# Some subtractions moved from VectorE to GpSimd, half loads paired in one buffer, and four copies issued later, in a one-core encoder layer on Trainium2

## The chip, the cores and the metric

The kernel runs on one core of one Trainium2 chip. The metric is the device time of one execution in microseconds (us). Three runs of the kernel before took 1076.27, 1076.62 and 1076.83; the median is 1076.62. Engine names are those of the profile: PE is TensorE's matmul, PEld its weight load, DVE is VectorE, ACT is ScalarE, POOL is GpSimd, SP is SyncE, which here only issues DMAs. PSUM is the memory that PE accumulates into, in banks of 128 x 512 floats; SBUF is the memory of the other tiles.

## The reference

One encoder layer over 1024 tokens with 1024 features, in float32. The input is normed and projected; the columns feed two token mixers side by side (group A: windowed grouped-query attention with a sink; group B: neighbourhood attention on a 16 x 64 grid). Each mixer's output is normed and both go through one output projection, with a residual. Then comes a gated MLP with 2816 hidden features, and a final norm. What the change touches is mostly the MLP's first half:

```python
def conv_gated_mlp(h, w_gate, w_up, conv_w, conv_b, w_down):
    g = jnp.einsum('bsd,df->bsf', h, w_gate)
    u = jnp.einsum('bsd,df->bsf', h, w_up)
    g = lax.conv_general_dilated(g, conv_w[:, None, :], ..., feature_group_count=D_FF) + conv_b
    return jnp.einsum('bsf,fd->bsd', jax.nn.silu(g) * u, w_down)
...
    h = h + jnp.einsum('bse,ed->bsd', mix, w_out[l])
    hn = rmsnorm(h, norm_ffn[l])
    h = h + conv_gated_mlp(hn, w_gate[l], w_up[l], conv_w[l], conv_b[l], w_down[l])
```

## The kernel before

**Precision by splitting.** Each float32 operand is split into a high part, rounded by ACT (`whi`, `hg`), and a low part, the rest, which VectorE subtracts (`wlo`, the second half of `hg`). A product of two operands is three matmuls: high x high, high x low and low x high (`group`, L957: L959, L960, L961; in the attention part `block`, L169). Weights come by a DMA on SP's queue into a tile `raw`; `split_w` (L943) makes the halves: L948 on ACT, L949 on VectorE. Inputs of the MLP are split by `operand` (L963: L966 on ACT, L967 on VectorE).

**Fewer products.** The MLP's products are blocked 2 x 2: tokens in two halves of 512, the 1024 features in two halves of four blocks of 128 (`K1` is blocks 0 to 3, `K2` blocks 4 to 7). Seven products of blocks replace eight, so sums and differences of the blocks are needed. `at(k, h)` is block k, half h, of the normed input. Of the first four blocks VectorE computes, in place, by `sub` (L998), the four sums that the names `t1` to `t4` stand for: t1 (L1181) and t2 (L1191) into `at(k, 1)`, then in one loop t3 (L1198) into `at(k, 0)` and t4 (L1199) into `at(k, 1)`. The last loop has eight subtractions of 128 x 512.

**Units.** A unit (class `Gated`, L1090) is one tile of 128 hidden features, gate and up together. It has seven products of 12 matmuls each: p1 and p2 into bank x, p5 and then p3 into bank y, p6, p7 and p4 into bank z. Where a second product goes into the same bank, it accumulates onto the first, so the instruction that reads the bank between them has to be done: L1100 and L1105 on ACT for x, L1110 and L1121 on VectorE for y, L1117, L1134 and L1139 on VectorE for z. The centred convolution is L1127 on ACT and L1128 and L1129 on VectorE, SiLU is L1130, the product of gate and up L1140.

**The head.** The first four units (`FO[:HEAD]`; here units 0 to 3) are run product by product: p1 and p2 of each, then p5 of all four (L1193), p6 of all four (L1200), p3, p7 and p4. Their weights come one product at a time (`head_weights`, L1002): a half of w_gate or of w_up, 256 KB, by `load_raw` (L952) into a tile `raw`, of which there are three of 512 KB size; a half load uses one whole tile. s1, s2, s4 and s3 are combinations of the halves and "22" is a half as it is. `sub` forms them in the tiles `ws`.

**The loop.** The other units (L1290; here unit 4, unit 5 and so on) go one after the other: p1, p5, p4 of the unit before, p6, p2, p3, convolution, p7. The steps of the next unit's weights (class `Weights`, L1045) stand between the products; its two loads are of 512 KB.

**Keeping.** When a unit's gate and up are multiplied, `keep` (L1153) stores the tile `c` of 512 KB to DRAM by a DMA on ACT's queue (L1155); `sums` (L1159) does the same for combinations of a pair of units. They are read back for the last part, the product with w_down.

**The output projection.** In the attention part the projections are jobs that fill PE between the attention's steps. A job's `load` is called one job ahead and `load_rest` at its twelfth step (`REST`, L757). `OutA` (L591) is the output projection of group A, eight jobs; its `load` fetches 256 KB and splits them at once (`load_w`, L166: L162 on ACT, L163 on VectorE), and its `load_rest` does nothing.

**What sets the order.** PE's instructions stand in the order of the program text (L128). Those of ACT, VectorE, GpSimd and SP are put in order by a scheduler when the program is built, by what it expects them to take; `behind` (L145) forbids it to put an instruction ahead of a named one, and `tc.high_priority` moves some forward. Each engine then works its list strictly in order, and a DMA is issued by the engine on whose queue it stands. A tile taken from a pool waits until the readers of its last user are done; `op` has 14 tiles (`c` and `cv` among them), `raw` three.

Of the kernel before, what the change touches and what calls it, by code (L numbers as in the profile page):

```python
# [13 lines left out]
F32 = mybir.dt.float32  # L14
F32R = mybir.dt.float32r
AF = mybir.ActivationFunctionType
ALU = mybir.AluOpType
# [3 lines left out]
KT = D // 128  # L21
NB = S // 128
HALF = 512
# [30 lines left out]
def hybrid_layer(tc, xT, w_first, w_in, w_out, w_gate, w_up, w_down, small, sink, rpb, consts, rope, out):  # L54
    nc = tc.nc
    with ExitStack() as ctx:
# [40 lines left out]
        for name, dst, n in (("h", his, 2), ("h", his, 2), ("l", los, 2), ("l", los, 2), ("w", None, 2)):  # L97
            t = flat(big(name, "mix", F32R)[:, :], n)
# [44 lines left out]
        mark = {}  # L143

        def behind(*names):  # L145

            stack = ExitStack()
            for n in names:
                stack.enter_context(tc.issue_after(mark[n].ins))
            return stack  # L150

        def fetch_w(src):

            raw = wpool.tile([128, 4, 128], F32, name="raw", tag="raw", bufs=2)
            nc.sync.dma_start(raw, src)
            return raw

        def halve_w(raw, held=False):

            hi, lo = (wpool.tile([128, 4, 128], F32R, name=n, tag=n) for n in ("whi", "wlo"))  # L160
            with behind(*["high", "rest"] * held):
                mark["weights"] = nc.scalar.activation(hi, raw, AF.Copy)  # L162
                mark["weights low"] = nc.vector.tensor_tensor(lo, raw, f32(hi[:, :, :]), op=ALU.subtract)  # L163
            return [(hi[:, j, :], lo[:, j, :]) for j in range(4)]

        def load_w(src):  # L166
            return halve_w(fetch_w(src), True)
# [422 lines left out]

        class OutA:  # L591
            def __init__(self, d):
                self.d = d

            def load(self):
                self.w = load_w(w_out[self.d, :, 0:4, :])

            def load_rest(self):
                pass

            def run(self):
                d = self.d
# [72 lines left out]
        t = quarters(big("f", "mix"))  # L675
# [5 lines left out]
        for part in range(3):  # L681
            for p, ps in zip(first, banks):
                w, x = p.w[0], xg[0]
# [129 lines left out]
        for g in range(2):  # L813
            for b in range(NB):
                q, t = unit_window(g, b)
# [53 lines left out]
        for u in range(len(flat)):  # L869
            q, t, need, kind = flat[u]  # L870
# [81 lines left out]
        def load_raw(src, n):  # L952
            raw = fpool.tile([128, n, 128], F32, name="raw", tag="raw", bufs=3, padded_shape=[128, KT, 128])
            nc.sync.dma_start(raw, src)
            return raw

        def group(ps, ws, xs, first, last):  # L957
            for i, (w, x) in enumerate(zip(ws, xs, strict=True)):
                nc.tensor.matmul(ps, w[0], x[0], start=first and i == 0, stop=False, skip_group_check=True)  # L959
                nc.tensor.matmul(ps, w[0], x[1], start=False, stop=False, skip_group_check=True)  # L960
                nc.tensor.matmul(ps, w[1], x[0], start=False, stop=last and i == len(ws) - 1, skip_group_check=True)  # L961
# [33 lines left out]
        HEAD = 4  # L995
        FH = FT // 2
        FO = [f for k in range(FH) for f in (k, k + FH)]
        sub = lambda o, x, y: nc.vector.tensor_tensor(o, x, y, op=ALU.subtract)  # L998

        wsum = [fpool.tile([128, 4, 128], F32, name="ws", tag="tt", bufs=6) for _ in range(HEAD)]  # L1000

        def head_weights(i, name):  # L1002
            f, t = FO[i], wsum[i]
            if name == "s1":
                u = load_raw(w_up[f], KT)
                nc.vector.tensor_tensor(t, u[:, 0:4], u[:, 4:8], op=ALU.add)
            elif name == "s2":
                g = load_raw(w_gate[f, :, 0:4], 4)
                sub(t, t, g)
            elif name == "s4":  # L1010
                g = load_raw(w_gate[f, :, 4:8], 4)
                sub(t, g, t)
            elif name == "s3":
                g, u = load_raw(w_gate[f, :, 0:4], 4), load_raw(w_up[f, :, 0:4], 4)
                sub(t, g, u)
            else:
                t = load_raw(w_up[f, :, 4:8], 4)
            W[f, name] = split_w(t, 4)

        for h in range(2):  # L1020
# [69 lines left out]
        class Gated:  # L1090
# [11 lines left out]
            def p2(self):  # L1102
                group(self.x, W[self.f, "12"], B[2, 1], False, True)
                self.gs = self.gs or big("gs", "mix")
                nc.scalar.activation(self.gs[:, 0:HALF], self.x, AF.Copy)  # L1105

            def p5(self):
                self.y = bank("y", self.tags[0])
# [27 lines left out]
            def p4(self):  # L1136
                group(self.z, W[self.f, "22"], B["t4"], False, True)
                u = self.c
                nc.vector.tensor_tensor(u[:, 0:HALF], self.z, u[:, 0:HALF], op=ALU.add)  # L1139
                nc.vector.tensor_tensor(u, u, self.cv, op=ALU.mult)  # L1140
                k = self.f % FH
                if self.f < FH:
                    first_of[k] = u
                    sub(u[:, HALF:S], u[:, HALF:S], u[:, 0:HALF])
                    keep(u, ("11", k), ("t1", k))
                else:
                    keep(u, ("21", k), ("22", k))


        FH = FT // 2  # L1150
        X, first_of = {}, {}

        def keep(t, *names):  # L1153
            d = dram.tile([128, HALF * len(names)], F32, name="x", tag="x" + "_".join(f"{n}{k}" for n, k in names))
            nc.scalar.dma_start(d, t)  # L1155
            for i, name in enumerate(names):
                X[name] = d[:, i * HALF:(i + 1) * HALF]
# [37 lines left out]
            head_weights(i, "s2")  # L1195
        B[2, 2] = [operand(at(k, 1), "op") for k in K2]
        for k in K1:
            sub(at(k, 0), at(k, 1), at(k, 0))  # L1198
            sub(at(k, 1), at(k + 4, 0), at(k, 1))  # L1199
        for i, u in enumerate(units):  # L1200
            u.p6()
            head_weights(i, "s4")
# [87 lines left out]
        for i, f in enumerate(FO[HEAD:]):  # L1290
            u = Gated(f)
            w_next.step(9)
            last_one = i + 1 == FT - HEAD
            w_next = None if last_one else Weights(FO[HEAD + i + 1])
            more = lambda n=1: w_next.step(n) if w_next else None
            more()
            u.p1()
            more()
            u.p5()
            if pend:  # L1300
                pend.p4()
# [12 lines left out]
            u.p2()  # L1314
            more()
            if last_one:
                for k in range(4, 6):
                    x_load(0, k)
                u.p7()
            u.p3()  # L1320
            u.conv()
            if last_one:
                prepare(3, 1)
            more()
            if not last_one:
# [241 lines left out]
```

## Time and profile before

| what | value |
| --- | --- |
| median of three runs | 1076.62 us |
| the profiled execution | 1076.77 us |
| its span, first to last instruction | 1075.0 us |
| mean granted clock of PE | 0.997 |
| PE busy | 99% of the span, 5094 matmuls |
| VectorE busy | 81%, 1596 instructions |
| ACT busy | 52%, 1059 instructions |
| GpSimd busy | 10%, 188 instructions |
| DMA | 144.94 MB, mean 135 GB/s |

The page of the profile gives sums over the whole span. The views by stretch, by wait and in order of time tell what holds PE in one stage. In the rows in order of time the columns are: start in us from the span's start, duration in us, engine, line of the kernel, operation, output <- inputs, shapes and count; in brackets stands how long the engine was idle before and what ended that. Instructions overlap a little at their ends, so on an engine that never idles the step from one start to the next is less than the duration shown. A row of a DMA on SP (SPq) is its issue, not its transfer. The head of the MLP with its units 0 to 3 runs from about 391 to 509 us, the loop follows, and the product with w_down ends the kernel.

### The profile page before, as it was taken

What the parts mean: (1) busy time and instruction counts of PE and PEld (TensorE: products, weight loads), DVE (VectorE), ACT (ScalarE), POOL (GpSimd) and SP (SyncE); (2) the same over time, 40 slices, a digit from 0 to 9 for tenths busy, and PEclk for the clock granted to TensorE, in tenths of its full rate; (3) what the DMA queues carried; (4) which work ended last, traced back from release to release, by engine and by line L of the source; (5) the groups of instructions that cost most, each with busy time, mean ns of one, the idle gap of its engine ahead of it and who ended that gap; (6) DMA issues with size and microseconds to landing.
All of it is one profiled execution on the core that took longest, in us unless ns stands there. A gap on an engine that the chain in (4) does not pass through costs nothing.

```text
span 1075.0 us, 14902 instructions
## 1 busy us (share of the span) xinstructions
PE 1063.8 (99%) x5094; PEld 889.6 (83%) x5094; DVE 867.3 (81%) x1596; ACT 555.7 (52%) x1059; POOL 106.8 (10%) x188
## 2 busy tenths in 40 slices
PE   9999999999999999999999999999999999999997
PEld 7888888888888888887788888888888888888887
DVE  7889887768878799899988877887887858897765
ACT  8457776647676554534434343432434645544451
POOL 1124333222332000000000000000000000000002
PEclk9999999999999999999999999999999999999998
DMA  7223122322234245214342232322222788867644
GB/s 278 74 74 80 40 69 60 89 69 79 78 88 148 96 156 210 78 56 162 135 157 98 106 110 81 129 106 108 98 89 101 251 288 308 270 216 241 222 139 157
DMA packets 68220, 144.94 MB, mean 135 GB/s; under 512 B 8240, under 2 KB 18736, under 8 KB 68144
## 3 DMA queue, kind: packets, MB, share of 16 engines
q1 hardware_dynamic: 57920, 118.69, 34.9%
q10 hardware_dynamic: 10224, 25.30, 6.2%
q8 instruction: 40, 0.66, 0.2%
q14 instruction: 36, 0.29, 0.1%
HBM read 103.58 MB, written 28.57 MB: 123 GB/s over the span
## 4 chain that ended last, share of the span: by engine, by line
PE 89%; DVE 7%; ACT 1%; issue 1%; DMA 1%; POOL 0%; SPq 0%; DVEq 0%; ACTq 0%
PE pj L170 8%; PE pj L172 8%; PE pj L171 8%; PE dn L959 7%; PE dn L961 7%; PE dn L960 7%; PE z L961 5%; PE z L959 5%; PE z L960 5%; PE s L381 3%; PE x L959 3%; PE x L961 3%; PE x L960 3%; PE y L961 3%; PE y L959 3%; PE y L960 3%
## 5 line engine op out<-in xcount | busy, mean ns | idle before, releaser
L948 ACT ACTIVATE whi<-ws 128x512 fp32r<-128x512 f32 (+1 forms) x100 | 60.3, 623 | 126.8 <-DVE ws L1066 82.5
L959 PE MATMUL dn<-xd,whi 128*128 128x512 f32 (+1 forms) x330 | 124.0, 376 | 0.0
L961 PE MATMUL dn<-xd,wlo 128*128 128x512 f32 (+1 forms) x330 | 123.7, 375 | 0.0
L960 PE MATMUL dn<-xd,whi 128*128 128x512 f32 (+1 forms) x330 | 123.7, 375 | 0.0
L961 PE MATMUL z<-hg,wlo 128*128 128x512 f32 x264 | 103.1, 390 | 0.9 <-DVE wlo L949 0.7
L170 PE MATMUL pj<-xgh,whi 128*128 128x512 f32 x245 | 103.3, 422 | 0.0
L959 PE MATMUL z<-hg,whi 128*128 128x512 f32 x264 | 103.0, 390 | 0.0
L960 PE MATMUL z<-hg,whi 128*128 128x512 f32 x264 | 102.8, 389 | 0.0
L407 ACT ACTIVATE p<-p,nm 128x385 f32<-128x385 f32 (+3 forms) x128 | 75.2, 587 | 50.8 <-DVE nm L403 49.7
L411 POOL TENSOR_SCALAR p<-p,sm 128x384 f32<-128x384 f32 (+1 forms) x128 | 78.1, 622 | 207.2 <-DVE sm L409 171.7
L171 PE MATMUL pj<-xgl,whi 128*128 128x512 f32 x245 | 96.2, 393 | 0.3 <-DVE xgl L626 0.3
L172 PE MATMUL pj<-xgh,wlo 128*128 128x512 f32 x245 | 96.4, 393 | 0.0
L949 DVE TENSOR_TENSOR wlo<-raw,whi 128x512 fp32r<-128x512 f32 (+1 forms) x102 | 66.4, 671 | 26.6 <-ACT whi L948 25.6
L418 DVE TENSOR_TENSOR pl<-pt,ph 128x384 fp32r<-128x384 f32 (+2 forms) x108 | 63.5, 589 | 24.9 <-ACT ph L417 23.5
L948 ACT ACTIVATE whi<-raw 128x512 fp32r<-128x512 f32 (+1 forms) x102 | 60.5, 612 | 44.6 <-DMA raw<-in_w_down_dram 19.8
L949 DVE TENSOR_TENSOR wlo<-ws,whi 128x512 fp32r<-128x512 f32 (+1 forms) x100 | 67.0, 683 | 19.1 <-ACT whi L948 17.9
L1384 POOL TENSOR_TENSOR h<-h,wide 128x256 f32<-128x256 f32 (+1 forms) x6 | 5.4, 918 | 707.4 <-ACT wide L1380 707.4
L417 ACT ACTIVATE ph<-pt 128x384 fp32r<-128x384 f32 (+2 forms) x108 | 55.2, 512 | 32.4 <-PE pt L517 24.7
L961 PEld LDWEIGHTS dn<-xd,wlo 128*128 128x128 f32 x330 | 62.1, 188 | 11.2
L960 PEld LDWEIGHTS dn<-xd,whi 128*128 128x128 f32 x330 | 62.1, 188 | 11.2
L959 PEld LDWEIGHTS dn<-xd,whi 128*128 128x128 f32 x330 | 62.1, 188 | 10.9
L1274 ACT ACTIVATE xd<-xd 128x512 fp32r<-128x512 f32 x77 | 47.6, 626 | 43.8 <-DMA xd<-x 42.1
(270 smaller groups left out, 2678.0 us busy)
## 6 DMA issues: line engine op xcount, KB each, us to landing
xd<-x SPq DMA_DIRECT2D x77, 256.0 KB, 4.8
raw<-in_w_down_dram SPq DMA_DIRECT2D x72, 256.0 KB, 3.8
raw<-in_w_gate_dram SPq DMA_DIRECT2D x22, 512.0 KB, 3.5
raw<-in_w_up_dram SPq DMA_DIRECT2D x22, 512.0 KB, 3.9
x<-c ACTq DMA_DIRECT2D x22, 512.0 KB, 3.3
raw<-in_w_in_dram SPq DMA_DIRECT2D x30, 256.0 KB, 2.8
raw<-in_w_down_dram SPq DMA_DIRECT2D x36, 192.0 KB, 4.2
x<-t ACTq DMA_DIRECT2D x11, 512.0 KB, 2.7
```

The costliest lines, as they stand in the source:

```text
L170: nc.tensor.matmul(ps, w[0], x[0][:, tsl(h)], start=first, stop=False)
L171: nc.tensor.matmul(ps, w[0], x[1][:, tsl(h)], start=False, stop=False)
L172: nc.tensor.matmul(ps, w[1], x[0][:, tsl(h)], start=False, stop=last)
L407: nc.scalar.activation(p[:, j, 0:e], p[:, j, 0:e], AF.Exp, bias=nm, scale=-1.0, accum_out=sm[:, j:j + 1])
L411: nc.gpsimd.tensor_scalar(p[:, i, 0:m], p[:, i, 0:m], sm[:, i:i + 1], 1.0, op0=ALU.mult, op1=ALU.mult)
L417: mark["high"] = nc.scalar.activation(ph[:, 0:n], ps[:, 0:n], AF.Copy)
L418: mark["rest"] = nc.vector.tensor_tensor(pl[:, 0:n], ps[:, 0:n], f32(ph[:, 0:n]), op=ALU.subtract)
L948: nc.scalar.activation(hi, src, AF.Copy)
L949: nc.vector.tensor_tensor(lo, src, f32(hi[:, :, :]), op=ALU.subtract)
L959: nc.tensor.matmul(ps, w[0], x[0], start=first and i == 0, stop=False, skip_group_check=True)
L960: nc.tensor.matmul(ps, w[0], x[1], start=False, stop=False, skip_group_check=True)
L961: nc.tensor.matmul(ps, w[1], x[0], start=False, stop=last and i == len(ws) - 1, skip_group_check=True)
```

## The change

- The loop that computes t3 and t4 names GpSimd for its eight subtractions; `sub` gets the engine as an argument.
- `head_weights` loads the halves of s2, s4, s3 and "22" by a new `load_half`: two of them share a `raw` tile of 512 KB, each in its half. The loads of s1, which are of full size, stay.
- `keep` for the first four units is put off: `p4` appends it to a list, and the loop takes two from the list in each unit, after p2, behind the copy of bank x (L1105, which gets the mark "joined").
- `OutA.load` only fetches for the first of its eight jobs; the split is then made in `load_rest`. For the others it is made at once, as before.

The order of PE's instructions is the same in both programs.

```diff
         class OutA:
             def __init__(self, d):
-                self.d = d
+                self.d, self.w = d, None
 
             def load(self):
-                self.w = load_w(w_out[self.d, :, 0:4, :])
+                self.raw = fetch_w(w_out[self.d, :, 0:4, :])
+                if self.d:
+                    self.load_rest()
 
             def load_rest(self):
-                pass
+                if not self.w:
+                    self.w = halve_w(self.raw, True)
...
+        free = []
+
+        def load_half(src):
+
+            if not free:
+                raw = fpool.tile([128, KT, 128], F32, name="raw", tag="raw", bufs=3)
+                free.extend([raw[:, 0:4], raw[:, 4:8]])
+            t = free.pop(0)
+            nc.sync.dma_start(t, src)
+            return t
...
-        sub = lambda o, x, y: nc.vector.tensor_tensor(o, x, y, op=ALU.subtract)
+        sub = lambda o, x, y, engine=nc.vector: engine.tensor_tensor(o, x, y, op=ALU.subtract)
...
             elif name == "s2":
-                g = load_raw(w_gate[f, :, 0:4], 4)
+                g = load_half(w_gate[f, :, 0:4])
                 sub(t, t, g)
             elif name == "s4":
-                g = load_raw(w_gate[f, :, 4:8], 4)
+                g = load_half(w_gate[f, :, 4:8])
                 sub(t, g, t)
             elif name == "s3":
-                g, u = load_raw(w_gate[f, :, 0:4], 4), load_raw(w_up[f, :, 0:4], 4)
+                g, u = load_half(w_gate[f, :, 0:4]), load_half(w_up[f, :, 0:4])
                 sub(t, g, u)
             else:
-                t = load_raw(w_up[f, :, 4:8], 4)
+                t = load_half(w_up[f, :, 4:8])
...
-                nc.scalar.activation(self.gs[:, 0:HALF], self.x, AF.Copy)
+                mark["joined"] = nc.scalar.activation(self.gs[:, 0:HALF], self.x, AF.Copy)
...
-                    keep(u, ("11", k), ("t1", k))
+                    names = ("11", k), ("t1", k)
                 else:
-                    keep(u, ("21", k), ("22", k))
+                    names = ("21", k), ("22", k)
+                if self.f in FO[:HEAD]:
+                    to_keep.append(lambda: keep(u, *names))
+                else:
+                    keep(u, *names)
...
         for k in K1:
-            sub(at(k, 0), at(k, 1), at(k, 0))
-            sub(at(k, 1), at(k + 4, 0), at(k, 1))
+            sub(at(k, 0), at(k, 1), at(k, 0), nc.gpsimd)
+            sub(at(k, 1), at(k + 4, 0), at(k, 1), nc.gpsimd)
...
             more()
             u.p2()
+            for _ in range(min(2, len(to_keep))):
+                with behind("joined"):
+                    to_keep.pop(0)()
             more()
```

More of the change, by code (lines that the diff above doesn't have):

```diff
@@ L1144, in p4 @@
                     sub(u[:, HALF:S], u[:, HALF:S], u[:, 0:HALF])
-                    keep(u, ("11", k), ("t1", k))
+                    names = ("11", k), ("t1", k)
                 else:
-                    keep(u, ("21", k), ("22", k))
+                    names = ("21", k), ("22", k)
[3 more added lines that the diff above has]
+                    keep(u, *names)
         FH = FT // 2
-        X, first_of = {}, {}
+        X, first_of, to_keep = {}, {}, []
         def keep(t, *names):
```

## The prediction

> **What bounds the kernel now.** First the page: its span and the engines' busy times.
>
> ```profile
> span 1075.0 us, 14902 instructions
> ...
> PE 1063.8 (99%) x5094; PEld 889.6 (83%) x5094; DVE 867.3 (81%) x1596; ACT 555.7 (52%) x1059; POOL 106.8 (10%) x188
> ```
>
> The profiled execution took 1076.77 us, 1.77 more than its span and 0.15 more than the median, 1076.62. TensorE bounds it, and a change that leaves its matmuls alone can only remove stalls between them. Where they stand is seen by comparing stretches (columns: us, then busy time and instructions of each engine, granted clock, DMA share, GB/s).
>
> ```profile
> 464.28:486.04 21.76, 21.76 (x98) 18.02 (x96) 21.76 (x35) 9.72 (x14) 0.00 (x0) 1.00 0.22 72
> 486.04:532.73 46.69, 45.38 (x193) 35.49 (x192) 43.90 (x61) 22.82 (x32) 0.00 (x0) 1.00 0.44 158
> 535.00:840.00 305.00, 305.00 (x1347) 252.57 (x1346) 246.29 (x346) 120.90 (x184) 0.00 (x0) 1.00 0.32 111
> ```
>
> The first stretch holds p6 and p3 of the four head units: eight groups of 12, so 21.76 / 96 = 0.2267 us per matmul. The second goes from p7 of the first head unit to the end of p5 of unit 5 (the second after the head), 16 groups, 192 x 0.2267 = 43.52; it took 46.69. So **3.17 us** of stall, 0.3% of the time, stand there. The third, the loop, has none (1347 x 0.2267 = 305), and VectorE is 81% busy in it. The waits of PE name the releaser, and two rows show one stall (between starts 0.73 instead of 0.23).
>
> ```profile
> PE z L961 <- DVE wlo L949: 0.7, 2, 0.4
> ...
> PE y L961 <- DVE wlo L949: 0.5, 2, 0.3
> ```
>
> ```profile
> 495.05 0.40 PE L960 MATMUL z<-hg,whi 128*128 128x512 f32 x1
> 495.78 0.50 PE L961 MATMUL z<-hg,wlo 128*128 128x512 f32 x1 [0.34 <-DVE wlo L949]
> ```
>
> PE waits for the low halves of weights, which VectorE makes. VectorE is late because it is full (the third busy time, 39.14 of 39.14 us), and for a bit because of loads:
>
> ```profile
> 453.90:493.04 39.14, 39.03 (x173) 31.97 (x171) 39.14 (x62) 17.77 (x27) 0.00 (x0) 1.00 0.21 68
> ```
>
> ```profile
> 453.90 1.89 DVE L998 TENSOR_TENSOR h<-h,h 128x512 f32<-128x512 f32 x3
> ...
> 465.31 1.30 DVE L998 TENSOR_TENSOR h<-h 128x512 f32<-128x512 f32 x2
> ...
> 468.92 1.30 DVE L998 TENSOR_TENSOR h<-h,h 128x512 f32<-128x512 f32 x2
> 470.13 0.70 DVE L1117 TENSOR_TENSOR gs<-z,c 128x512 f32<-128x512 f32 x1
> ...
> 493.24 0.69 DVE L998 TENSOR_TENSOR ws<-raw 128x512 f32<-128x512 f32 x1 [0.20 <-DMA raw<-in_w_up_dram]
> ...
> 497.44 1.38 DVE L949 TENSOR_TENSOR wlo<-raw,whi 128x512 fp32r<-128x512 f32 x2 [0.51 <-ACT whi L948]
> ...
> 499.78 0.69 DVE L949 TENSOR_TENSOR wlo<-raw,whi 128x512 fp32r<-128x512 f32 x1 [0.36 <-ACT whi L948]
> 501.11 0.69 DVE L1139 TENSOR_TENSOR c<-z,c 128x512 f32<-128x512 f32 x1 [0.63 <-PE z L961]
> ...
> 517.84 0.68 DVE L1110 TENSOR_TENSOR c<-y,c 128x512 f32<-128x512 f32 x1
> 518.43 1.22 DVE L1140 TENSOR_TENSOR c<-c,cv 128x1024 f32<-128x1024 f32 x1
> 519.57 1.29 DVE L949 TENSOR_TENSOR wlo<-ws,whi 128x512 fp32r<-128x512 f32 x2
> ```
>
> The eight subtractions that move are the block from 465.31 to 470.13: 4.82 us, 0.60 each. From there to 517.84 VectorE idles only in the four places shown, 0.20 + 0.51 + 0.36 + 0.63 = 1.70.
>
> **The change part by part.** Every count of instructions and every order below is that of the two built programs; PE's order is the same in both.
>
> *The subtractions on GpSimd.* They free 4.82 us of VectorE. What they cost on the other side:
>
> ```profile
> 1050.07 2.55 POOL L1384 TENSOR_TENSOR h<-h,wide 128x512 f32<-128x512 f32 x2 [691.90 <-ACT wide L1380]
> ```
>
> ```profile
> 1050.02 4.04 DVE L1386 SCALAR_TENSOR_TENSOR h<-h,par,sw 128x512 f32<-128x512 f32 x6 [0.38 <-ACT wide L1380]
> ```
>
> 1.28 us each, 10.2 for eight, on an engine with nothing to do from 358 to 1050. The first needs t2 of block 0 (the row at 453.90, written by 454.5), so alone they would end by 465; their results are wanted by p7 at 486 and p4. But VectorE need not run freely beside them. L1386 above, which reads one operand from PSUM (sw), kept 0.67 per instruction. Instructions that read both operands from SBUF did not:
>
> ```profile
> 248.17 0.99 POOL L481 TENSOR_TENSOR xb<-cst,rr 128x384 f32<-128x384 f32 x1 [1.18 <-DVE nm L403]
> 249.12 1.17 POOL L482 TENSOR_TENSOR xb<-cst,rr 128x256 f32<-128x256 f32 x1
> ```
>
> ```profile
> 244.65 0.69 DVE L163 TENSOR_TENSOR wlo<-raw,whi 128x512 fp32r<-128x512 f32 x1
> ...
> 248.22 1.50 DVE L163 TENSOR_TENSOR wlo<-raw,whi 128x512 fp32r<-128x512 f32 x1
> 249.63 1.21 DVE L299 SCALAR_TENSOR_TENSOR kb<-t,cst,ka 128x512 fp32r<-128x512 f32 x1
> ...
> 251.30 0.73 DVE L299 SCALAR_TENSOR_TENSOR kb<-t,cst,ka 128x512 fp32r<-128x512 f32 x1
> ```
>
> L163 took 1.50 instead of 0.69 beside the 384-wide GpSimd instruction, 0.81 more; then GpSimd waited (1.17); then L299 lost 0.48 to its 256 columns. They take turns. At 0.48 + 0.33 per further 128 columns, or 0.81/0.99 of 1.28, a 512-wide one costs VectorE 1.05 to 1.14. L163's pitch has about 0.07 of slack beyond its own reading, so I take **1.0** for each that meets such an instruction, and 0.4 (1.0 less 0.6) where an instruction reading PSUM runs beside it. GpSimd does the first subtraction of blocks 0 to 2, the second of 0 to 2, then both of block 3. Walking down both queues with one GpSimd instruction between two of VectorE's, its 1st to 5th and 7th each meet a subtraction for t2 (L998) or a split L967, SBUF only; the 6th and 8th run beside two L1110, which read y from PSUM. Lost: 6 x 1.0 + 2 x 0.4 = **6.8 us** against 4.82 freed: VectorE is 2.0 later, not earlier. (Bounds of the loss: 0, if all were like L1386; 9.0, with 1.28 and 0.68.) New waits: the splits of t3 and t4 on ACT and VectorE wait for GpSimd, and behind them stand the weight splits of s4 and s3; GpSimd would be done by 468, and VectorE comes to the first of them at about 477, so it waits for none.
>
> [...]
>
> *Two loads in one raw buffer.* SyncE now waits on single buffers:
>
> ```profile
> 434.03 38.95 SPq L954 DMA_DIRECT2D raw<-in_w_gate_dram  x8
> ...
> 490.06 6.62 SPq L954 DMA_DIRECT2D raw<-in_w_up_dram  x5
> ```
>
> Twenty half loads use ten buffers instead of twenty, so each can be asked for about one buffer earlier, and the loads of unit 4 behind them too. The waits for data go: the 0.20, the 0.51 and 0.36 (ACT's whi waits for the same loads), and the 0.63 for PE, since VectorE is later than PE there. That is worth **1.70** of VectorE. New: unit 4's w_up, in the slot of the first "22" pair, and ACT's split of its s2; about 0.5 and 0.65, **1.15** (the load, the first row below, lands 3.9 us after the slot comes free; bounds 0 to 2).
>
> ```profile
> raw<-in_w_up_dram SPq DMA_DIRECT2D x22, 512.0 KB, 3.9
> ...
> x<-c ACTq DMA_DIRECT2D x22, 512.0 KB, 3.3
> ```
>
> *VectorE's new order.* The scheduler moves unit 4's s1, s2, s4, s3 and "22" forward. That ends the stalls on wlo, all 3.17. But c<-y (L1110) of unit 4 now stands behind five instructions that came after it: four splits L949 and one L1140 (518.43 to 519.57), 4 x 0.60 + 1.14 = **3.54**. It matters because p3 accumulates into the bank y, which L1110 must have read:
>
> ```profile
> 521.30 0.39 PE L959 MATMUL y<-hg,whi 128*128 128x512 f32 x1
> ```
>
> ```profile
> 521.30:532.73 11.43, 11.14 (x49) 1.00 0.36 135
> ```
>
> From p3 of unit 4 to the end of unit 5's p5 stand 48 matmuls, 10.88, in 11.43: 0.55 of the 3.17 lie behind p3's start. Without the other 2.62, p3 would start at 518.68.
>
> *Deferred copies.* Four stores (x<-c above) leave their places among the head's work on ACT and follow L1105, two per loop unit. Their issue lies beside ACT's idle time (busy 22.82 of 46.69 in the second stretch): no cost; without that cover a third of a us each (SyncE's rows of one issue). A tile c is held until its store has landed, 3.3 us after p2 of unit 4, about 526; the first reuse of such a slot that I find, unit 5's c<-x, follows that unit's p1 at about 531. SyncE's queue is not touched. *First output weight.* On ACT and VectorE its split moves back by some 15 us, to just ahead of the L417 at 321.58:
>
> ```profile
> 306.34 0.63 ACT L162 ACTIVATE whi<-raw 128x512 fp32r<-128x512 f32 x1
> ...
> 321.58 0.49 ACT L417 ACTIVATE ph<-pt 128x384 fp32r<-128x384 f32 x1 [0.30 <-PE pt L517]
> ```
>
> ```profile
> 324.10 0.48 PE L170 MATMUL pj<-mgh,whi 128*128 128x512 f32 x1
> ...
> 324.64 0.40 PE L172 MATMUL pj<-mgh,wlo 128*128 128x512 f32 x1
> ```
>
> ACT waits 0.30 there, so the split is done by 321.9, its low half by 322.5, and L417 loses some 0.3; the halves are used at 324.10 and 324.64. PE waits on neither engine where the split stood or goes. I count nothing; one split, 0.63, if that cover is gone.
>
> **The sum.** c<-y of unit 4 starts at 517.84 - 4.82 + 6.8 - 1.70 + 1.15 + 3.54 = 522.8 and ends at 523.5; p3 starts there instead of at 521.30: +2.2. The stall at unit 5's p5 goes, since PE is later and its s1 is not: -0.55. Together **+1.6 us**, 1078.4 for the profiled execution, **1078.2** for a median. Each us of loss L on the port changes it by one, down to L = 2.0, where p3 is on time and -3.17 is all there is.
>
> **Rivals.** (a) *The port costs little* (L below 3.0): VectorE keeps the lead, wlo and c<-y are on time, -2.2 to -3.17, 1073.5. For it: several DVE instructions read PSUM; and GpSimd may find gaps. Against: L163 and L299, and that VectorE has no gap from 454 to 493. [...] (c) *The change doesn't do what it says*: the loads come no earlier, because the slots are freed by VectorE, which is later; then the 1.70 stays, 1079.9.
>
> ```profile
> 458.23 0.63 ACT L966 ACTIVATE hg<-h 128x512 fp32r<-128x512 f32 x1 [1.68 <-DVE h L998]
> ```
>
> **Chances.** Forecast (L from 3.0 to 7.3: within 0.2%, 2.15 us, about what a measurement of this kernel can tell from no change): 0.45. Slower, (b) with 0.24 and (c) with 0.10: 0.34. Faster, (a): 0.21. The range holds (a) at 1073.5 and (b) at 1080.4: 1073.3 to 1080.6, which leaves out what I have not thought of; the forecast's own is 1074.5 to 1078.8.
>
> **What would show it.** Right: GpSimd's eight subtractions take over 1.4 us each in the trace, L949, L967 and L998 near 455 to 468 over 1.2, no PE wait on wlo between 486 and 533, but one of about 4 us before the first y matmul of unit 4's p3, on L1110. Wrong: subtractions of 1.28 with L967 at 0.69 beside them (then (a)); a PE stall at 466 on hg (then (b)); any new wait in the loop after 535, or near 321, which I have at nothing.

## The result, and the profile after

The changed kernel takes **1080.34 us** (median of 6 runs, 1078.23 to 1081.61) where the kernel before took 1076.44 beside it: a ratio of 1.0034 with a 95% interval of 1.0024 to 1.0044, some 3.7 us slower (the two medians differ by 3.9). That lies inside the predicted range (1073.3 to 1080.6), 0.3 from its upper end, but not in the forecast's own case (1074.5 to 1078.8): the time is the one that rival (b) gave, 1080.4. The execution profiled took 1081.61, the longest of the six.

The page's line of busy times, and then a comparison of stretches (us, busy time and instructions of PE, PEld, DVE, ACT and POOL, granted clock, DMA share, GB/s), of the changed kernel:

```profile
PE 1065.2 (99%) x5094; PEld 890.9 (83%) x5094; DVE 866.5 (80%) x1588; ACT 554.7 (51%) x1059; POOL 122.1 (11%) x196
```

```profile
540.00:845.00 305.00, 305.00 (x1347) 252.55 (x1346) 245.43 (x344) 119.92 (x182) 0.00 (x0) 1.00 0.31 113
525.80:529.20 3.40, 3.40 (x10) 2.63 (x9) 3.37 (x6) 0.35 (x1) 0.00 (x0) 0.50 0.44 173
465.04:537.76 72.72, 68.11 (x290) 54.88 (x288) 69.25 (x96) 30.20 (x43) 4.82 (x4) 0.98 0.27 98
```

VectorE has eight instructions less and GpSimd eight more. The loop still has no stall: 305.00 busy of 305.00. The loss is in the stretch from p6 of the first head unit to the end of unit 5's p5: 72.72, where the same matmuls took 21.76 + 46.69 = 68.45 before, 4.27 more. And for 3.4 us of it TensorE had half its clock, which no stretch of the kernel before shows there. What PE waited for in that stretch (us, times, longest):

```profile
PE y L973 <- DVE c L1124: 2.2, 1, 2.2
PE x L973 <- ACT c L1114: 1.6, 1, 1.6
PE y L975 <- DVE wlo L952: 0.6, 1, 0.6
PE z L975 <- DVE wlo L952: 0.2, 1, 0.2
```

None of the four waits on wlo of before, which stood in p7 of the last head unit and in units 4 and 5, is left. Two others on wlo have come, both at the first low half of a product of the head: in p3 (477.15, 0.75 beyond the usual step from start to start) and in p4 (499.39, 0.33). Two long waits are new, both in unit 4: ahead of p2 and ahead of p3. PE's own rows around the long ones, with the last start before each:

```profile
517.88 0.39 PE L975 MATMUL z<-hg,wlo 128*128 128x512 f32 x1
519.89 0.50 PE L973 MATMUL x<-hg,whi 128*128 128x512 f32 x1 [1.62 <-ACT c L1114]
...
522.52 0.39 PE L975 MATMUL x<-hg,wlo 128*128 128x512 f32 x1
525.14 0.50 PE L973 MATMUL y<-hg,whi 128*128 128x512 f32 x1 [2.23 <-DVE c L1124]
```

The first stall is 519.89 - 517.88 less the usual 0.23, 1.78; the second 2.39. Behind the second, from 526.04 to 529.03, starts stand 0.43 apart instead of 0.23: that is the half clock of the row above. p3 waits for c<-y (L1124, L1110 of before), as forecast. Why it is late is seen on VectorE:

```profile
459.20 1.18 DVE L952 TENSOR_TENSOR wlo<-ws,whi 128x512 fp32r<-128x512 f32 x1
465.26 1.82 DVE L981 TENSOR_TENSOR hg<-h,hg 128x512 fp32r<-128x512 f32 x1 [4.88 <-ACT hg L980]
467.00 0.68 DVE L1124 TENSOR_TENSOR c<-y,c 128x512 f32<-128x512 f32 x1
467.60 2.88 DVE L952 TENSOR_TENSOR wlo<-ws,whi 128x512 fp32r<-128x512 f32 x2
```

```profile
523.26 1.22 DVE L1154 TENSOR_TENSOR c<-c,cv 128x1024 f32<-128x1024 f32 x1
524.40 0.69 DVE L1124 TENSOR_TENSOR c<-y,c 128x512 f32<-128x512 f32 x1
```

Four instructions with two operands in SBUF were stretched by 0.50, 1.14 and (two) 1.60, and VectorE idled 4.88 us for a split on ScalarE. ScalarE and GpSimd at that time:

```profile
459.86 0.63 ACT L980 ACTIVATE hg<-h 128x512 fp32r<-128x512 f32 x1 [2.82 <-POOL h L1012]
461.57 0.63 ACT L980 ACTIVATE hg<-h 128x512 fp32r<-128x512 f32 x1 [1.07 <-POOL h L1012]
464.07 1.16 ACT L980 ACTIVATE hg<-h 128x512 fp32r<-128x512 f32 x2 [1.87 <-POOL h L1012]
```

```profile
455.22 7.57 POOL L1012 TENSOR_TENSOR h<-h 128x512 f32<-128x512 f32 x3 [96.26 <-DVE h L1012]
462.76 3.77 POOL L1012 TENSOR_TENSOR h<-h,h 128x512 f32<-128x512 f32 x3
466.49 1.74 POOL L1012 TENSOR_TENSOR h<-h 128x512 f32<-128x512 f32 x1
468.31 1.62 POOL L1012 TENSOR_TENSOR h<-h,h 128x512 f32<-128x512 f32 x1
```

While VectorE idles, three take 3.77, 1.26 each; the first three took 7.57. The row of the line for the first kind gives their durations (ns: shortest, median, longest):

```profile
L1012 POOL TENSOR_TENSOR h<-h x4: 1293/1740/4612, 455.2 to 466.5; 128x512 f32<-128x512 f32 x4
```

The longest, 4.61 us, is the first: it was issued at 455.22 and got on only when VectorE came to an instruction that reads PSUM (c<-y at 458.60). ScalarE's split of t2's block 3, the second of the two at 464.07, stood behind three splits that wait for GpSimd.

### The profile page after: what moved, and what is told of

Read it like the earlier page. It is cut to its first block, busy times and chain, and to the rows that moved or that the text cites. A ratio compares the mean times of both kernels' runs of the same rounds, so it can differ in the third digit from the quotient of the medians.

```text
span 1079.8 us, 14907 instructions
## 1 busy us (share of the span) xinstructions
PE 1065.2 (99%) x5094; PEld 890.9 (83%) x5094; DVE 866.5 (80%) x1588; ACT 554.7 (51%) x1059; POOL 122.1 (11%) x196
## 4 chain that ended last, share of the span: by engine, by line
PE 89%; DVE 7%; issue 1%; ACT 1%; DMA 0%; POOL 0%; SPq 0%; DVEq 0%; ACTq 0%; POOLq 0%
PE pj L170 8%; PE pj L172 8%; PE pj L171 8%; PE dn L973 7%; PE dn L975 6%; PE dn L974 6%; PE z L973 5%; PE z L975 5%; PE z L974 5%; PE s L381 3%; PE x L973 3%; PE x L974 3%; PE x L975 3%; PE y L973 3%; PE y L975 3%; PE y L974 3%
## 5 line engine op out<-in xcount | busy, mean ns | idle before, releaser
L170 PE MATMUL pj<-xgh,whi 128*128 128x512 f32 x245 | 103.2, 421 | 0.0
L952 DVE TENSOR_TENSOR wlo<-raw,whi 128x512 fp32r<-128x512 f32 (+1 forms) x102 | 66.1, 671 | 25.7 <-ACT whi L951 24.9
L952 DVE TENSOR_TENSOR wlo<-ws,whi 128x512 fp32r<-128x512 f32 (+1 forms) x100 | 69.0, 702 | 19.7 <-ACT whi L951 18.3
L418 DVE TENSOR_TENSOR pl<-pt,ph 128x384 fp32r<-128x384 f32 (+2 forms) x108 | 63.5, 589 | 24.8 <-ACT ph L417 23.5
L417 ACT ACTIVATE ph<-pt 128x384 fp32r<-128x384 f32 (+2 forms) x108 | 55.3, 513 | 32.1 <-PE pt L517 24.4
L973 PE MATMUL y<-hg,whi 128*128 128x512 f32 x176 | 69.3, 394 | 2.2 <-DVE c L1124 2.2
```

Source lines behind the costliest of these rows:

```text
L170: nc.tensor.matmul(ps, w[0], x[0][:, tsl(h)], start=first, stop=False)
L417: mark["high"] = nc.scalar.activation(ph[:, 0:n], ps[:, 0:n], AF.Copy)
L418: mark["rest"] = nc.vector.tensor_tensor(pl[:, 0:n], ps[:, 0:n], f32(ph[:, 0:n]), op=ALU.subtract)
L952: nc.vector.tensor_tensor(lo, src, f32(hi[:, :, :]), op=ALU.subtract)
```

## The experiments

**Theory A**, formed from these rows: what costs is GpSimd's reading of SBUF beside a VectorE that is never idle, about 8 us of VectorE's time against 4.82 freed; through c<-y it becomes TensorE's stall. Rivals: the new order and the deferred copies cost, whoever subtracts; or the clock's drop alone, by chance. A subdivision: the loss is ScalarE's queue (A1), or the turns that VectorE and GpSimd take, whatever ScalarE does (A2).

The table gives the ratio of each to the kernel before, run beside it on the same chip, with its 95% interval, and, from each profile, the time from the first x matmul of the gated part to the first dn matmul, which start and end of the kernel don't disturb. Kernels were run in four sessions, so their times are compared by the ratios and not by the medians. For before and after its ends are these rows:

```profile
430.70 0.39 PE L959 MATMUL x<-hg,whi 128*128 128x512 f32 x1
...
853.80 0.39 PE L959 MATMUL dn<-xd,whi 128*128 128x512 f32 x1
```

```profile
431.46 0.39 PE L973 MATMUL x<-hg,whi 128*128 128x512 f32 x1
...
859.07 0.39 PE L973 MATMUL dn<-xd,whi 128*128 128x512 f32 x1
```

| kernel | median us | ratio to before | x to dn us |
|---|---|---|---|
| before | 1076.44, 1076.47, 1076.11, 1075.98 | 1 | 423.1 |
| after | 1080.34 | 1.0034 (1.0024 to 1.0044) | 427.6 |
| after, run again | 1080.69 | 1.0040 (1.0026 to 1.0054) | 427.3 |
| after, subtractions on VectorE | 1074.50 | 0.9982 (0.9974 to 0.9991) | 421.4 |
| before, subtractions on GpSimd | 1083.63 | 1.0067 (1.0054 to 1.0079) | 430.6 |
| after, output weight as before | 1081.12 | 1.0046 (1.0033 to 1.0060) | 427.7 |
| after, t3 and t4 splits held back | 1079.46 | 1.0031 (1.0020 to 1.0043) | 426.5 |
| after, memsets on GpSimd (t3 and t4 left out) | 1073.63 | 0.9974 (0.9963 to 0.9984) | 419.8 |
| after, copies on GpSimd (t3 and t4 left out) | 1074.51 | 0.9986 (0.9978 to 0.9995) | 420.9 |
| after, unit 4's c<-y earlier | 1077.90 | 1.0017 (1.0008 to 1.0026) | 424.2 |
| half loads and deferred copies | 1073.92 | 0.9977 (0.9968 to 0.9986) | 421.0 |
| half loads alone | 1074.56 | 0.9983 (0.9974 to 0.9992) | 421.0 |
| later output split alone | 1076.28 | 1.0002 (0.9994 to 1.0011) | 422.9 |

**After, with the subtractions on VectorE.**

```
-            sub(at(k, 0), at(k, 1), at(k, 0), nc.gpsimd)
-            sub(at(k, 1), at(k + 4, 0), at(k, 1), nc.gpsimd)
+            sub(at(k, 0), at(k, 1), at(k, 0))
+            sub(at(k, 1), at(k + 4, 0), at(k, 1))
```

> The changed kernel with its eight subtractions back on VectorE; the half loads, the deferred copies and the output weight as changed. Theory A (GpSimd's subtractions are what costs: they take VectorE some 7 us between 455 and 466, against 4.8 that they free, and with that make c<-x and c<-y of unit 4 late): the stall of 2.4 us ahead of p3 of unit 4, the 1.8 ahead of its p2 and the half clock behind them are gone, 0.4 of the output weight's wait near 325 stays; 1073.5 to 1075, 2 to 3 us below before. Rival B (VectorE's order and the deferral cost, whoever subtracts: c<-y of unit 4 behind five later instructions): still 1078 or more. Rival C (only the drop of the granted clock costs, and it comes by chance): about 1077.

1074.50, as theory A has it; in the x to dn stretch 6.2 us less than after. Its waits of PE from 464 to 540:

```profile
PE y L975 <- DVE wlo L952: 0.3, 1, 0.3
PE z L973 <- DVE gs L1131: 0.2, 1, 0.2
```

Both long stalls are gone, and so is the half clock. The scheduler also puts unit 4's c<-y ahead of three L952 and one L1154 that stand before it in after (3 x 0.60 + 1.14 = 2.9 us); whether the order or GpSimd is to blame is told apart by the memsets, below.

**Before, with the subtractions alone on GpSimd.** The edit is the opposite of the one above, in the kernel before.

> The kernel before with only its eight subtractions put on GpSimd; loads, copies and output weight as before. Theory A: VectorE loses some 7 us between 455 and 466 as in the changed kernel, c<-y of unit 4 stands behind the same five instructions and starts later still, since the waits for loads (1.70) stay: the head's stalls as in the changed kernel or up to 1.5 us more, none at 325; 1079.5 to 1082. Rival B (the half loads' and the deferral's order cost): 1076 to 1077.5, no stall over 1 us ahead of p3 of unit 4. By the forecast's own sum (loss 6.8): 4.82 freed, so 2.0 later plus 3.54: p3 some 3.9 later, about 1080.

1083.63: theory A's sign, but more than it gave. c<-y of unit 4 starts at 526.81, 2.4 later than after (3.1 later counted from the first x matmul, which comes at 430.77 here and at 431.46 there). PE's waits from 464 to 540, and VectorE's from 480 to 530:

```profile
PE y L959 <- DVE c L1110: 3.3, 1, 3.3
PE z L959 <- ACT whi L948: 2.2, 1, 2.2
```

```profile
DVE wlo L949 <- ACT whi L948: 2.9, 3, 2.0
DVE ws L998 <- DMA raw<-in_w_up_dram: 0.7, 1, 0.7
```

VectorE waits 3.6 us for loads and what follows them, where before it waited 1.1 (0.9 and 0.2 by the same lines of before). With VectorE late, the raw buffers come free late too; the half loads, which the changed kernel has, take these waits away. PE's 2.2 on whi, ahead of a matmul at 495.15, comes from the same late loads. So the parts are not additive: the half loads bring 2.2 us where they stand with the deferred copies, and about 3 beside the subtractions on GpSimd (430.6 against 427.7 from x to dn, the second being after with the output weight as before).

**After, with the t3 and t4 splits held back.**

```
         B["t2"] = []
         ...
+        mark["halved2"] = mark["halved"]
         ...
-        B["t3"] = [operand(at(k, 0), "op") for k in K1]
+        with behind("halved2"):
+            B["t3"] = [operand(at(k, 0), "op") for k in K1]
         ...
-            B["t4"].append(operand(at(k, 1), "mix" if k else "rstd"))
+            with behind("halved2"):
+                B["t4"].append(operand(at(k, 1), "mix" if k else "rstd"))
```

("halved" marks ScalarE's half of each split.)

> The changed kernel with ScalarE's and VectorE's splits of t3 and t4 held behind the last split of t2, so that ScalarE no longer stands at a wait for GpSimd ahead of the split of t2's block 3. VectorE idles 4.88 us there in the changed kernel. Theory A1 (the larger part of the loss is this queue on ScalarE): that idle time shrinks to under 1 us, c<-y of unit 4 starts 3 to 4 us earlier, p3 of unit 4 is on time or nearly, and the clock does not drop: 1075 to 1077. Rival A2 (the shared port costs whatever ScalarE does: GpSimd, kept out by VectorE for 2.5 us an instruction, then meets VectorE's later work and makes it wait in its turn): GpSimd's work ends later and VectorE's instructions beside it stretch by the same 4 to 5 us; 1079 to 1081.

1079.46. PE's two long waits stay (2.2 and 1.5). The idle 4.88 is gone, but not the loss. VectorE's rows:

```profile
459.74 1.19 DVE L952 TENSOR_TENSOR wlo<-ws,whi 128x512 fp32r<-128x512 f32 x1
460.85 1.77 DVE L981 TENSOR_TENSOR hg<-h,hg 128x512 fp32r<-128x512 f32 x1
462.55 0.68 DVE L1124 TENSOR_TENSOR c<-y,c 128x512 f32<-128x512 f32 x1
463.15 2.88 DVE L952 TENSOR_TENSOR wlo<-ws,whi 128x512 fp32r<-128x512 f32 x2
465.95 1.77 DVE L981 TENSOR_TENSOR hg<-h,hg 128x512 fp32r<-128x512 f32 x1
...
468.25 4.58 DVE L981 TENSOR_TENSOR hg<-h,hg 128x512 fp32r<-128x512 f32 x3
472.75 0.68 DVE L1124 TENSOR_TENSOR c<-y,c 128x512 f32<-128x512 f32 x1
```

Taken by their starts, with 0.60 as the undisturbed pitch, the five rows with two SBUF operands (eight instructions) lose 0.5, 1.1, 1.6, 1.1 and 2.7 us, **7.0** in all for eight of GpSimd; the c<-y between them, which read PSUM, lose nothing. A2 holds: where ScalarE no longer makes VectorE wait, VectorE and GpSimd take turns, and pay nearly the same. ScalarE's queue is worth the difference, 8.1 - 7.0 = 1.1 us, the amount by which the x to dn time fell (427.6 to 426.5). A1 falls.

**After, with memsets on GpSimd.**

```
-            sub(at(k, 0), at(k, 1), at(k, 0), nc.gpsimd)
-            sub(at(k, 1), at(k + 4, 0), at(k, 1), nc.gpsimd)
+            nc.gpsimd.memset(at(k, 0), 0.0)
+            nc.gpsimd.memset(at(k, 1), 0.0)
```

> The changed kernel with GpSimd's eight subtractions replaced by eight memsets of the same tiles, in the same places: GpSimd writes the tiles and reads nothing (the third and fourth sums are left out of the computation). VectorE's order, with c<-y of unit 4 behind five later instructions, and ScalarE's queue stay as in the changed kernel. Theory A (the subtractions' reading on GpSimd is what makes VectorE's instructions beside it wait): VectorE's instructions between 455 and 470 keep their 0.60, the wait on ScalarE is under 1 us, c<-y starts near 517, p3 of unit 4 is on time: 1073.5 to 1075.5. Rival (any work of GpSimd beside VectorE costs as much, or the scheduler's order does): 1078 to 1081.

1073.63, and no wait of PE at all from 440 to 545. A row of GpSimd, and VectorE's beside it:

```profile
457.00 1.73 POOL L1217 MEMSET h<- 128x512 f32 x3 [5.07 <-DVE hg L981]
```

```profile
456.26 1.88 DVE L981 TENSOR_TENSOR hg<-h,hg 128x512 fp32r<-128x512 f32 x3
458.07 0.68 DVE L1012 TENSOR_TENSOR h<-h,h 128x512 f32<-128x512 f32 x1
458.67 0.68 DVE L1124 TENSOR_TENSOR c<-y,c 128x512 f32<-128x512 f32 x1
```

Beside memsets VectorE keeps its 0.60. c<-y of unit 4, behind the same five instructions as after, starts at 516.83, 7.6 earlier than after, and nobody waits for it. So the order alone costs nothing; it costs because VectorE is late. (The memsets are shorter than the subtractions, 0.53 against 1.28, and some run earlier; that doesn't touch this reading.)

**After, with copies on GpSimd.** In place of the memsets, `nc.gpsimd.tensor_copy(at(k, 0), at(k, 1))` and `nc.gpsimd.tensor_copy(at(k, 1), at(k + 4, 0))`.

> The changed kernel with GpSimd's eight subtractions replaced by eight copies of one tile each (each reads one operand from SBUF instead of two; the third and fourth sums are left out of the computation). All orders as in the changed kernel. If any reading of SBUF by GpSimd takes turns with VectorE's two-operand instructions: VectorE's instructions beside a copy stretch by about the copy's own duration, and the first copy waits behind seven back-to-back instructions as the first subtraction did (4.6 us); 1077 to 1081. If it takes two operands: VectorE keeps its 0.60, as beside the memsets, and p3 of unit 4 is on time: 1073.5 to 1075.

1074.51: by the time the second case, by the trace the first. GpSimd's and VectorE's rows:

```profile
454.49 5.53 POOL L1216 COPY h<-h 128x512 f32<-128x512 f32 x3 [96.27 <-DVE h L1012]
459.97 1.74 POOL L1217 COPY h<-h 128x512 f32<-128x512 f32 x3
```

```profile
458.49 1.05 DVE L952 TENSOR_TENSOR wlo<-ws,whi 128x512 fp32r<-128x512 f32 x1
461.80 1.00 DVE L981 TENSOR_TENSOR hg<-h,hg 128x512 fp32r<-128x512 f32 x1 [2.26 <-ACT hg L980]
```

One operand read is enough: the first three copies took 5.53 where three take 1.74, VectorE's instruction stretched from 0.68 to 1.05, and ScalarE's queue made VectorE idle 2.26. But a copy takes 0.6 and not 1.28, so c<-y starts at 518.85 and 0.7 of wait is left ahead of p3. Where I expected that reading would cost 1077 or more, I had the mechanism and not the size.

**After, with unit 4's c<-y earlier.** p5 takes a priority, and the first unit of the loop passes 500:

```
-            def p5(self):
+            def p5(self, urgent=0):
                 ...
-                nc.vector.tensor_tensor(self.c[:, HALF:S], self.y, self.c[:, 0:HALF], op=ALU.add)
+                with tc.high_priority(offset=urgent):
+                    nc.vector.tensor_tensor(self.c[:, HALF:S], self.y, self.c[:, 0:HALF], op=ALU.add)
```

> The changed kernel with c<-y of unit 4 given a higher priority, which puts it ahead of three of VectorE's five instructions that it stands behind (one L1153, one L952, one L1154: 0.60 + 0.60 + 1.14 = 2.34). If the stall of 2.39 ahead of p3 of unit 4 comes from this order: under 0.2 left of it, the 1.78 ahead of p2 stays. If the half clock for 3.4 us behind it (some 1.4 lost) is the long stall's work, it goes too: 1.4 + 2.3 below the changed kernel, 1076.5; if the clock drops anyway, 1078. If the order isn't what makes p3 late (another wait comes last): 1080.

1077.90, a ratio of 1.0017 where after has 1.0034, so some 1.8 us below after. c<-y starts at 521.44, the wait ahead of p3 is gone, the 1.6 ahead of p2 and the two on wlo stay, and a wait of 0.5 on gs (L1132) comes new ahead of unit 4's p7. In this profile the clock is whole from 520 to 527:

```profile
520.00:527.00 7.00, 6.48 (x28) 4.78 (x28) 6.97 (x12) 1.41 (x2) 0.00 (x0) 1.00 0.47 148
```

From x to dn it gains 3.4: the 2.39 and the clock's 1.6, less the new 0.7. Given that VectorE is late, the order makes p3 late, and the drop goes with the stall. The time fell by less than the 3.4; the run profiled of after was its slowest.

**After, with the output weight as before; and the later output split alone.** The one takes the diff's OutA part back, the other makes it alone.

> The changed kernel with the first output weight loaded and split as before. If its late split costs the 0.43 us that stand ahead of the matmuls at 324 and 326 in the changed kernel: 0.4 less than the changed kernel, no wait there, the rest alike. If that wait has another cause (startup, the offset of the whole trace): the same time, and the wait stays.

> The kernel before with the later split of the first output weight alone. If the waits of 0.14 and 0.27 near 324 and 326, which stand in every kernel with this edit and in none without, aren't taken back later: 0.4 above before, 1076.5 to 1076.9 where before is 1076.1 to 1076.5. If a later wait takes them back: the same as before, within 0.2.

The times don't resolve 0.4: the first is 1.0046, not below after's 1.0034 (the intervals overlap), the second 1.0002 with 0.9994 to 1.0011. The traces agree with each other: the wait below (after's) stands in each of the eight profiles with the later split, and in none of the five without it; a shorter one stands ahead of the pj at 324. Counted from start to start, from an L170 just ahead (323.07 in after) to the one behind both waits (327.58), 4.49 to 4.52 us pass in the eight and 3.96 or 3.97 in the five.

```profile
326.60 0.33 PE L528 MATMUL o<-ph,v 128*128 128x384 f32 x1
327.16 0.45 PE L529 MATMUL o<-pl,v 128*128 128x384 f32 x1 [0.23 <-DVE pl L418]
```

So PE loses 0.54 there, a little more than the 0.43 of the expectations. That this reaches the end isn't shown.

**Half loads with deferred copies, and half loads alone.**

> The changed kernel with its subtractions on VectorE and the first output weight as before: half loads and deferred copies alone. If the late split of the output weight costs its 0.43 us near 325 in every run: 1074.1, 0.4 below the kernel that differs by it alone (1074.5). If not (0.4 lies within what other waits take back): 1074.5.

> The kernel before with the half loads alone. If the deferred copies cost and bring nothing, as forecast: within 0.4 of the kernel with half loads and deferred copies, about 1074.3. Rival: the gain on before (1.9 us with half loads, deferred copies and output weight) comes from the copies, that leave ScalarE free: then this one is at 1076 or more.

1073.92 and 1074.56, and from x to dn 421.0 in both: the deferred copies neither cost nor bring anything there, and the half loads make the gain (the two ratios, 0.9977 and 0.9983, have intervals that overlap). The first is **the fastest kernel that computes everything**, 2.2 us below before (0.9977, 0.9968 to 0.9986).

**After, run again.**

> The changed kernel itself once more. If the half clock behind the 2.4 us stall ahead of p3 of unit 4 is that stall's work: it is there again, 3.4 us long from about 525.5, in this trace too, and the time is 1080 to 1081.5. If it came by chance in the first profile: full clock there, and a span 1.4 shorter (1078.4).

1080.69, with both long waits again and the half clock at the second. The granted clock of a stretch is the third figure from its end; the 0.56 below is a mean: 0.44 of 3.40 us is what 2.99 us at half clock lose, so by estimate the drop ended near 528.6:

```profile
525.60:529.00 3.40, 3.40 (x10) 2.64 (x10) 3.37 (x7) 0.01 (x1) 0.00 (x0) 0.56 0.48 193
```

The drop is no chance of one run. It came in all five profiles in which PE waited 2.2 us or more ahead of p3, a stall of 2.4 or more (after, after again, output weight as before and splits held back with a wait of 2.2, before with the subtractions on GpSimd with 3.3; over 510 to 535 the splits held back have a mean clock of 0.93, as after has). The clock was 1.00 from 510 to 535 in before and with the subtractions on VectorE, and from 520 to 533 with the memsets, with c<-y earlier and with half loads and deferred copies; the longest wait of PE in these five was 1.6. But length alone doesn't decide. Before with the subtractions on GpSimd has a second stall of 2.4 us, the one on whi (a wait of 2.2), which ends at 495.15, and the clock stays whole behind it. Two stretches around that stall and two around the one ahead of p3:

```profile
491.40:494.81 3.41, 1.54 (x7) 0.94 (x5) 3.41 (x5) 3.38 (x4) 0.00 (x0) 1.00 0.28 74
494.81:498.23 3.42, 2.60 (x10) 1.87 (x11) 3.42 (x6) 1.98 (x4) 0.00 (x0) 1.00 0.21 80
525.54:528.95 3.41, 1.40 (x6) 1.19 (x7) 3.41 (x6) 0.60 (x1) 0.00 (x0) 1.00 0.82 294
528.95:532.36 3.41, 3.41 (x10) 2.62 (x9) 2.69 (x5) 0.63 (x1) 0.00 (x0) 0.50 0.49 192
```

What differs from profile to profile in the same code is a wait ahead of L233 near 416: none in before and after, 0.65 here, 0.92 with the splits held back. It is one part of the spread of the runs.

## Why the prediction was right, and where it was wrong

The start of c<-y, counted from VectorE's block of t2 subtractions (453.90 before, 454.38 after), term by term:

| step | forecast us | measured us |
|---|---|---|
| subtractions freed, 8 x 0.60 | -4.82 | -4.82 |
| c<-y behind four L952 and one L1154 more | +3.54 | +3.54 |
| loss L beside GpSimd | +6.8 | +8.1 = 4.88 + 0.50 + 1.14 + 1.60 |
| waits for loads | -0.55 | -0.8, the remainder |
| c<-y of unit 4 later | +4.96 | +6.08 (70.02 less 63.94) |
| p3 of unit 4 later | +2.2 | +3.1 (3.84 less 0.76 of offset) |
| behind p3 without the clock | -0.55 | -0.4 (12.62 less 11.43, less 1.6) |
| half clock | not counted | +1.6 (7 x 0.20 and two of 0.1) |
| output weight | nothing | +0.54 |

The +1.6 of the sum became 3.1 - 0.4 + 1.6 + 0.54 = 4.8, close to the 4.84 by which the two profiled executions differ (1081.61 and 1076.77).

- **What bounds it, and which wait is last**: right. The stalls of 486 to 533 were what the change moved, wlo's waits went as forecast in units 4 and 5, and c<-y ahead of p3 took their place, by the five instructions that the order shows. Not all stalls on wlo ended: the one at 499.39 lies where none was to be, and the one at 477.15 in a stretch that had no stall before. Neither matters for p3's start, which c<-y sets.
- **The loss L: mis-sized.** 6.8 was forecast, 8.1 came. That lies beyond 7.3, the upper end of the forecast's own L, where the chances go over to rival (b). With the queue on ScalarE out of the way it was 7.0, near the 6.8, but partly by luck: eight instructions lost 0.88 each in the mean, where the forecast had six at 1.0 and two at 0.4 beside PSUM readers. The 1.0 was an estimate from the rows of L163 and L299, and the 0.07 of slack in it no run shows; in after the four instructions lost 0.50, 1.14 and 0.80 each of two. Nor does any run show the port on which the prediction and the expectations put the loss: what they show is that VectorE's instructions with two operands in SBUF and GpSimd's that read SBUF lengthen each other (GpSimd's 1.28 became 4.61 at most). The step that failed was "so it waits for none". It looked at VectorE's own queue, where the first split that needs GpSimd's results comes at about 477. ScalarE has three of these splits ahead of that of t2's block 3; the third waits for GpSimd's fourth subtraction until 464.04, and VectorE idles 4.88 us behind it. In before the split of t2's block 3 stood at 458.23, behind 1.68 of waiting for VectorE (the prediction's last row).
- **Turns**: wrong at the start. The forecast had GpSimd's instructions meet VectorE's one by one from 455. VectorE's seven instructions from 454.38 to 458.60 ran at 0.60, and GpSimd's first waited through all of them. Only from there did they take turns. That first one ended at 459.83 instead of about 456.5 (455.22 + 1.28), and the fourth, which ScalarE waits for, came later with it.
- **Rival (b)**, a loss at the upper bound of 9.0: right that the change is slower; wrong in the stall on hg, at 466 by the forecast, that was to show it. p6 starts at 465.04 in after and by the forecast's 0.2267 per matmul wants the split of t2's block 3 at 465.04 + 10 x 0.2267 = 467.31; it ended at 467.08, 0.2 earlier, and PE has no stall there. That the measured time is (b)'s 1080.4 is partly luck: by the prediction's sum an L of 8.1 gives 1079.5, and the clock and the output weight, which no case had, bring the rest.
- **Rival (a)** fell, by the memsets above all: that is what L = 0 would look like, and it gives 1073.6, the 1073.5 of the forecast. **Rival (c)** fell for the changed kernel; its condition, that VectorE's lateness holds the buffers back, shows in the subtractions on GpSimd alone.
- **The output weight, counted at nothing**: wrong by 0.54. L417 and L163 were seen to shift by 0.3, and that L418, behind them, feeds PE at once wasn't followed.
- **The clock**: not foreseen. The forecast priced the stall at its length; it cost 1.6 us on top. The stall of 1.78 ahead of p2 wasn't in the forecast either. It isn't needed for the drop: before with the subtractions on GpSimd has only one of 0.4 there, and a longer one ahead of p3, 3.5, and the clock drops. ScalarE's c<-x waits for a slot that VectorE's L1154 frees:

```profile
519.24 0.60 ACT L1114 ACTIVATE c<-x 128x512 f32<-128x512 f32 x1 [1.41 <-DVE c L1154]
```

It is the same lateness seen 5 us earlier. As p3 waits for c<-y in any case, it adds nothing to p3's start.

- **The signs** came in part: four of GpSimd's eight subtractions took over 1.4 us and four 1.28 or 1.29, which ran while VectorE idled or stood blocked; and the stall ahead of p3 was 2.4 and not about 4, as 1.78 of the lateness showed ahead of p2.

## What to carry to other kernels

Before work goes from a full VectorE to an idle GpSimd, count both prices beside each other: here 0.60 us was freed and 0.9 to 1.0 lost for each instruction, because what ran beside it read two operands from SBUF; instructions that read PSUM lost nothing (0.68 beside the subtractions), nor did any beside memsets on GpSimd (0.60 from start to start). Then look at the in-order queues of the third engines: one split that waits for the slower engine holds up those behind it. And a stall of TensorE can cost more than its length: here those of 2.4 us or more ahead of p3 did in every profile (1.6 us on top in after), one of 1.8 didn't, and neither did one of 2.4 that fell differently in time.

## What the runs showed of the hardware

**A GpSimd instruction waited through a run of VectorE's.** A GpSimd subtraction issued at the second of seven two-operand VectorE instructions took 4.61 us (after) instead of 1.28, and 4.62 with the splits held back; with copies the first three took 5.53 instead of 1.74. In after it ended at 459.83, 1.23 behind the start of the first VectorE instruction that read PSUM (c<-y at 458.60): it was held up past the end of the instruction that it met, through the rest of an unbroken run. After that VectorE waited for GpSimd in its turn, 0.5 to 1.1 us an instruction and 0.88 in the mean (7.0 for eight, splits held back). Beside memsets, which read nothing, VectorE kept its 0.60.

**Half the clock after a stall of 2.4 us.** TensorE's granted clock went to 0.50 for 3.41 us in after, from 525.80 to 529.21, beginning 0.66 us after work had begun again (525.14). In the 3.41 us ahead of that, from 522.39, PE was busy for 1.18 and idle for 2.23. A single wait of 1.6, a stall of some 1.8, had no such effect in the kernel with c<-y earlier (1.00 from 520 to 533). The times at which the clock changed are regular in the two traces of before and after: in before the first drop, at 1067.785, lies 1061.545 us behind the first record of the full clock (6.240), in after, at 525.798, 518.826 behind it (6.972), and the next one there, at 1075.343, 549.545 behind the first. These are 311, 152 and 161 times 3.4133, and the drop in after lasted 3.413.

Stretches of this length give a possible reason why one stall of 2.4 us costs and another doesn't. It is an estimate; no run was made to test it. Going by PE's busy time, the 3.41 us just ahead of a drop had 2.23 idle in after at 525.80 and 2.01 in before with the subtractions on GpSimd at 528.95 (3.41 less 1.40 in the rows above). The stall of 2.4 without a drop lies across two such stretches, which meet at 494.81 and have 1.87 and 0.82 idle (491.40 to 494.81 and 494.81 to 498.23 in the rows). This is an observation of these profiles and not a rule: at the end of before a drop follows 3.41 us with only 1.03 idle (1064.37 to 1067.78).
